# Expert row lists taken in two parts, the first two blocks started inside the routing, and the last two blocks added through a 0/1 product

## The chip, the cores and the metric

The kernel runs on one core of a Trainium2 chip. The metric is device time in microseconds (us) from launch to end; lower is better. Engines are named as in the profile: PE (TensorE matmuls) and PEld (its weight loads), DVE (VectorE), ACT (ScalarE), POOL (GpSimd), SP (SyncE, which issues most DMAs). Everything is float32 unless a tile says bf16.

## What is computed

One layer of a hybrid decoder on 512 prompt tokens and 8 decoding tokens: a mixer (attention and convolution), then a mixture of experts, then a last RMSNorm. The change touches only the part from the end of the mixer on:

```python
x = x + mods[2] * mix
h = rmsnorm(x, norm2_g) * (1.0 + mods[4]) + mods[3]
# hier_moe(h): softmax over 4 groups, top 1; top 2 of the 8 experts of that group
hid = silu(h @ w_gate[e]) * (h @ w_up[e])        # 1024 -> 256, each of 32 experts
y   = sum over the token's two experts of weight * (hid @ w_down[e])
x   = x + mods[5] * y
out = rmsnorm(x, final_g)
```

Each token has two (token, expert) pairs, 1040 in all. Every expert's weights are 3 MB (gate, up, down, 1 MB each), 32 experts, 96 MB.

## The kernel before, in words

**Mixer end.** Attention runs over four tiles of 128 tokens. Between its steps a written queue (`QUEUE`, `FILL`) slips in the output projection: `project(i, n)` (line 1250) makes half n of tile i's new x (`x1`), stores it to `xrow` in DRAM (line 1257), and adds up its squares; `rows(i)` (line 1272) then scales the tile by its 1/rms on ACT (line 1279), multiplies by `A2b` and adds `B2b` on POOL (lines 1280 and 1281), stores h to `hrow` in DRAM (line 1282), and calls `choose(i)` and `place(i)`.

**Routing.** `choose(i)` (line 1179) finds the two experts of each token of tile i on DVE as 0/1 rows `OH`, and has PE count how many earlier tokens chose each expert (`pps`, lines 1201 and 1202). `place(i)` (line 1204) turns that into a slot of a block of 64 rows: `Rs`, the 0/1 matrix of the slot within its block, and `kk`, `OH3`, for which block. After the last tile, lines 1437 to 1482 work out, from the counts of all experts, the table `T` of blocks: 52 blocks of 64 rows, of which the first 6 (`NF`) belong to fixed experts 26 to 31, the next eight to four experts with two blocks each (`HV`), 22 more to one expert each, and 16 spare ones are for what is left over, behind a branch. `px` (lines 1449 to 1454) is the PE product that sums the counts, copied at line 1464. Lines 1483 to 1499 make from this `gix`, the list of rows of `hrow` for each pair of blocks; `six` (line 1515) is where each row's result goes in `yrow`; `wtb` (line 1538) its weight; `exi` (line 1510) the number of the expert of each block, read by SP into a register (line 1570) to address the weight loads (line 1574).

**Blocks.** `run` (line 1646) goes through 36 blocks. For each pair of blocks `gather` (line 1584) fetches 128 rows from `hrow` by an indirect DMA from POOL, `turned` (line 1589) transposes them on PE in two halves, `up` (line 1601) multiplies by gate and up, `hidden` (line 1610) is Silu on ACT and a product on DVE, `flip` (line 1616) transposes, `down` (line 1625) multiplies by the down weights, scales by weight and mods[5] (line 1634, tile `ot`) and scatters the rows to `yrow` by an indirect DMA from POOL (line 1635). Block b's `down` comes after block b+1's `up`; a list `chain` fixes PE's order. Weights lie in a pool of 21 pages of 1 MB (`NPAGE`), which hold everything of that size: the six fixed experts are loaded ahead during attention (`fetch`, line 1061, 18 pages), the pages `mA`, `mB` hold h and its transposes, and `rt` the routing's tables. Each further expert takes three pages that have become free.

**End.** After the 36th block the 16 spare blocks stand behind a branch that is not taken with these inputs (`nxi`, lines 1688 and 1689). Then SP reads `yrow` back (line 1703: per tile of 128 tokens two halves of 0.5 MB, `yt`), DVE adds both to x (`xt`, lines 1712 and 1716), ACT sums the squares (line 1717), POOL takes the power -0.5 (line 1723), DVE scales (line 1735), and SP stores (line 1736). `sample` (line 1738) does the 8 decoding tokens on POOL.

The instructions of each engine stand in an order that the compiler's scheduler picks from the program's order and from its own estimate of when inputs are ready; each engine then works through its list strictly in order. `issue_after(x)` forces an instruction behind x on its engine.

Of the kernel before, what the change touches and what calls it, by code (L numbers as in the profile page):

```python
# [20 lines left out]
EPS = 1e-6  # L21
# [97 lines left out]
def layout(x):  # L119
# [57 lines left out]
    a["RC"] = _RC  # L177
    return a


def body(tc, I, O, dbg=lambda *a: None):
# [899 lines left out]
    yrow = dr.tile([4 * NT, 512], F32, name="yrow")  # L1081
    m5s = cp.tile([128, 256], F32, name="m5s")
# [77 lines left out]
    BO = box(3, 10, NBLK, half_=True)  # L1160
    OH3 = BO.rearrange("p f a b -> p (f a b)")[:, :960].rearrange("p (a b c) -> p a b c", a=10, b=3)
# [17 lines left out]
    def choose(i):  # L1179
# [17 lines left out]
        V.tensor_tensor(Cb[:, i], OH[:, i, 0], OH[:, i, 1], op=ALU.add)  # L1197
        pps[i] = tps("pps", (128, 32))
# [4 lines left out]

    def place(i):
        m = eb
        V.tensor_tensor(m, OH[:, i], pps[i].unsqueeze(1).to_broadcast([128, 2, 32]), op=ALU.mult)
        r, k, r_ = rk[:, 0, 2 * i:2 * i + 2], kk[:, 2 * i:2 * i + 2], rk[:, 1, 2 * i:2 * i + 2]
        V.tensor_reduce(r, m, axis=AX.X, op=ALU.add)
# [3 lines left out]
        for j in range(2):  # L1212
# [6 lines left out]
                        s3.unsqueeze(3).to_broadcast([128, 2, 3, 32]), op=ALU.mult)  # L1219
        V.scalar_tensor_tensor(k, k, -1.0, s3[:, :, 2], op0=ALU.mult, op1=ALU.mult)  # L1220
        if i == 4:
            V.tensor_scalar(k, k, K("inv"), None, op0=ALU.add)

# [26 lines left out]
    def project(i, n):  # L1250
# [5 lines left out]
        V.scalar_tensor_tensor(xh, pA, ra[:, 0, i:i + 1], xh, op0=ALU.mult, op1=ALU.add)  # L1256
        SP.dma_start(xrow[128 * i:128 * i + 128, 512 * n:512 * n + 512], xh)
# [14 lines left out]
    def rows(i):  # L1272
# [6 lines left out]
        hop = S.activation(h2, x1[i], AF.Copy, scale=rs2[:, i:i + 1])  # L1279
        G.tensor_tensor(h2, h2, A2b, op=ALU.mult)  # L1280
        G.tensor_tensor(h2, h2, B2b, op=ALU.add)
        SP.dma_start(hrow[128 * i:128 * i + 128, :], h2)
        choose(i)
        yield
        place(i)
# [38 lines left out]
    later = []  # L1324
    for i in range(4):
        if i < 3:
            split_q(i + 1)
        if i == WOC:
            load_wo(1, 3)
            w1_, w2_ = page("mA"), page("mB")  # L1330
            (m2b, A2b), (B2b, pqs) = [(half(t, 0), half(t, 1)) for t in (w1_, w2_)]
            h2b = [m2b, pqs]
# [104 lines left out]
    pct = tps("pct", (32, 1))  # L1437
# [16 lines left out]
    PE.matmul(px[:, 2, :], col(2), K("su")[:32, :33], start=True, stop=True)  # L1454
# [27 lines left out]
    V.scalar_tensor_tensor(T[:, 2], ov[:, :32], 1.0 - OV0, hB, op0=ALU.add, op1=ALU.add)  # L1482
# [294 lines left out]
```

## Time and profile before

| | us |
|---|---|
| median of three runs (804.25 to 809.23) | 806.44 |
| the profiled execution, own time | 798.72 |
| its span, first to last instruction | 796.9 |

Durations are from the profiled execution. PE is busy 88% of the span, DVE 56%, ACT and POOL 27% and 26%. The mean granted clock of TensorE is 0.938 of full speed. Times in rows are us from the span's start. The routing lies from about 497 to 525, the blocks from 524 to 760, the end from 760 to 797.

### The profile page before, as it was taken

To read this page: it belongs to the slowest core of one execution; us is meant where nothing else is said; L and a number is where in the kernel's file an instruction comes from. 1 tells how busy PE (TensorE), PEld (TensorE's weight loads), DVE (VectorE), ACT (ScalarE), POOL (GpSimd) and SP (SyncE) were. 2 spreads that over 40 slices of the span, in tenths; PEclk is the share of its full clock that TensorE was granted. 3 is DMA by queue.
4 is the path that set the end of the run, shared out by engine and by line. 5 is a ranking of instruction groups with operands and counts; after the bars stand their busy time and mean duration, and the time that the engine had idled before them with its cause. 6 is when DMAs were issued, how large, how long until landed. Compare 5 with 4: busy or idle time off the path is not lost. (4 is left out here: it accounts for less than half of the span.)

```text
span 796.9 us, 12648 instructions
## 1 busy us (share of the span) xinstructions
PE 698.6 (88%) x4888; PEld 419.3 (53%) x4888; DVE 443.9 (56%) x960; ACT 214.5 (27%) x491; POOL 210.8 (26%) x182
## 2 busy tenths in 40 slices
PE   4999898998969998999998998279999999999800
PEld 3555887876757446544443554255555555554400
DVE  3445629999973857553356757853333333333245
ACT  1254721211113447543435323110101101010011
POOL 5144205043202101014253034213222222321114
PEclk9999999999979998999997999579999999999965
DMA  9985325646867702520006575669999999999953
GB/s 344 419 332 201 135 80 214 240 159 238 271 238 303 278 2 76 229 106 1 0 2 239 199 276 206 243 204 410 419 416 351 402 419 418 417 420 419 368 196 152
DMA packets 42332, 200.02 MB, mean 251 GB/s; under 512 B 10733, under 2 KB 14205, under 8 KB 22677
## 3 DMA queue, kind: packets, MB, share of 16 engines
q1 hardware_dynamic: 29341, 156.27, 50.2%
q0 software_dynamic: 10336, 40.95, 13.2%
q10 hardware_dynamic: 2592, 1.95, 0.8%
q8 instruction: 40, 0.66, 0.3%
q14 instruction: 23, 0.19, 0.1%
HBM read 187.82 MB, written 22.15 MB: 263 GB/s over the span
## 5 line engine op out<-in xcount | busy, mean ns | idle before, releaser
L591 DVE SCALAR_TENSOR_TENSOR y<-u,c,y 128x511 f32<-128x511 f32 (+23 forms) x120 | 102.2, 884 | 2.1
L1613 ACT ACTIVATE hd<-pgu 64x256 f32<-64x256 f32 x36 | 13.6, 377 | 200.3 <-PE pgu L1608 200.3
L1635 POOL DMA_INDIRECT yrow<-ot,six x36 | 39.2, 1088 | 99.2 <-DVE ot L1634 87.6
L1608 PE MATMUL pgu<-eu,mB 128*64 128x256 f32 x256 | 61.8, 384 | 1.9 <-DMA eu<-in_WU 1.8
L1608 PE MATMUL pgu<-eg,mB 128*64 128x256 f32 x256 | 62.2, 384 | 0.0
L1630 PE MATMUL pd<-ed,hTe 128*64 128x512 f32 x240 | 57.3, 598 | 0.8 <-issue 0.8
L1608 PE MATMUL pgu<-eu,mA 128*64 128x256 f32 x224 | 54.0, 384 | 1.7 <-DMA eu<-in_WU 1.7
L1608 PE MATMUL pgu<-eg,mA 128*64 128x256 f32 x224 | 54.2, 384 | 0.0
L1634 DVE SCALAR_TENSOR_TENSOR ot<-pd,wtb,mt 128x512 f32<-128x512 f32 x36 | 27.0, 751 | 44.3 <-PE pd L1630 44.3
L1614 DVE TENSOR_TENSOR hd<-pgu,hd 64x256 f32<-64x256 f32 x36 | 15.4, 428 | 57.3 <-ACT hd L1613 57.3
L1608 PEld LDWEIGHTS pgu<-eg,mB 128*64 128x64 f32 x256 | 32.8, 136 | 19.8 <-issue 5.1
L225 DVE COPY hTe<-hTp 128x128 f32<-128x128 f32 x36 | 10.5, 292 | 50.1 <-PE hTp L1621 47.4
L1608 PEld LDWEIGHTS pgu<-eg,mA 128*64 128x64 f32 x224 | 28.9, 136 | 17.7 <-issue 5.2
L1367 DVE TENSOR_REDUCE ast<-pSp 128x1 f32<-128x384 f32 (+3 forms) x44 | 27.0, 633 | 20.1 <-PE pSp L1364 19.9
L1372 ACT ACTIVATE P<-pSp,ast 128x128 f32<-128x128 f32 (+3 forms) x64 | 33.1, 528 | 15.4 <-DVE ast L1367 13.7
L370 PE MATMUL pr<-cTs,wc 128*64 128x256 f32 x256 | 36.1, 390 | 0.0
L1608 PEld LDWEIGHTS pgu<-eu,mB 128*64 128x64 f32 x256 | 33.0, 137 | 3.9 <-DMA eu<-in_WU 2.8
L1253 PE MATMUL woA<-wo,qT 128*128 128x512 f32 x64 | 32.1, 606 | 0.0
L1391 PE MATMUL oT<-PTp,kv 128*64 128x512 f32 x80 | 31.9, 652 | 0.0
L1109 PE MATMUL woC<-wo,y 128*128 128x512 f32 x64 | 31.2, 605 | 0.0
L361 PE MATMUL cT<-CI,cR 128*128 128x128 f32 x128 | 21.1, 302 | 11.0 <-DVE cR L386 10.9
L1608 PEld LDWEIGHTS pgu<-eu,mA 128*64 128x64 f32 x224 | 28.9, 136 | 2.7 <-DMA eu<-in_WU 2.1
(572 smaller groups left out, 1680.2 us busy)
## 6 DMA issues: line engine op xcount, KB each, us to landing
eg<-in_WG SPq DMA_DIRECT2D x26, 1024.0 KB
eu<-in_WU SPq DMA_DIRECT2D x26, 1024.0 KB
ed<-in_WD SPq DMA_DIRECT2D x26, 1024.0 KB
wada<-in_WA SPq DMA_DIRECT2D x16, 1024.0 KB
wada<-in_WA POOLq DMA_DIRECT2D x8, 1024.0 KB
WG<-in_WG SPq DMA_DIRECT2D x6, 1024.0 KB
WU<-in_WU SPq DMA_DIRECT2D x6, 1024.0 KB
WD<-in_WD SPq DMA_DIRECT2D x6, 1024.0 KB
```

What stands on the lines that cost most here:

```text
L361: PE.transpose(p[:, j, :], R[b:b + n, c, k, 2 * s8:2 * s8 + 2, :], ident[b:b + n, b:b + n])
L370: mark["PE"] = PE.matmul(self.pr[r][64 * c:64 * c + 64], wc1[:, c, 8 * r + 4 * h + s, :], self.T[h][:, c, s], start=(h == 0 and s == 0), s ...
L591: V.scalar_tensor_tensor(yb[:, s_:CVS], ub[:, :CVS - s_], w(k), yb[:, s_:CVS], op0=ALU.mult, op1=ALU.add)
L1109: PE.matmul(p, zc[:, g, 128 * i:128 * i + 128], wo[2 * n + 1][:, g], start=(g == 0), stop=(g == 3))
L1253: PE.matmul(pA, oTp[:, g, 128 * i:128 * i + 128], wo[2 * n][:, g], start=(g == 0), stop=(g == 3))
L1367: V.tensor_reduce(st[k][:, 0, h0:h0 + nh], pS[k][:, :nh * L].rearrange("p (h l) -> p h l", h=nh), axis=AX.X, op=ALU.max, negate=True)
L1372: S.activation(P[k][:, g, :L], pS[k][:, o:o + L], AF.Exp, bias=st[k][:, 0, g:g + 1], accum_out=st[k][:, 1, g:g + 1])
L1391: PE.matmul(oT[64 * k:64 * k + 64, :], kv12[:, br - 1, kt, 128 + 64 * k:192 + 64 * k], PT[k], start=(br == 1 and kt == 0), stop=False)
L1608: chain[0] = PE.matmul(pgus[b][64 * h:64 * h + 64, :], xT[:, c, 64 * s_:64 * s_ + 64], w[:, c, :], start=(c == 0), stop=(c == 7))
L1630: chain[0] = PE.matmul(pd[64 * h:64 * h + 64, :], hT_[:, c, :], wd[:, c, 512 * h:512 * h + 512], start=(c == 0), stop=(c == 1))
L1634: V.scalar_tensor_tensor(ot, pd, wtb[:, b:b + 1], mt, op0=ALU.mult, op1=ALU.mult)
L1635: st = G.indirect_dma_start(out=yrow[:, :], out_offset=bass.IndirectOffsetOnAxis(ap=six[:, b:b + 1], axis=0), in_=ot, in_offset=None, boun ...
```

## The change

Six edits. (1) Only tiles 0 and 1 call `choose` and `place` as they go; `choose(2)` and `choose(3)` are called one after the other behind tile 3, and tile 3's h is made on PE: x times `A2b` beforehand (half on POOL, half on DVE), a diagonal matrix of the 1/rms, and `B2b` added by a one-row product. (2) The row lists of the six fixed experts (three pairs of blocks) are made by `static_part` and `static_rows` from tables `BS` of their own, straight after `choose(3)`, and the first gather is issued there. (3) PE transposes the first pair and runs `up(0)` between the parts of `px`, and `up(1)` behind the product for `exi`; `place(2)` and `place(3)` follow; `hidden(0)` stands behind `gix`, `hidden(1)` behind `wtb`. (4) `yrow` is filled with zeros early. (5) The branch stands behind `down` of block 33; `down` of blocks 34 and 35 keeps its rows in SBUF (`held`) instead of scattering them. (6) What the other blocks wrote is added to `xt` by eight DMAs from POOL with `accum_op=add`, issued behind the branch; the held rows are added by a PE product with a 0/1 matrix `oh` (token number against `tk`). Tile 3's 1/rms is made on ACT and DVE.

```diff
+            SP.dma_start(yrow.rearrange("(p a) (g f) -> p (a g) f", p=104, f=256), zr[:104].unsqueeze(1).to_broadcast([104, 40, 256]))
...
         V.scalar_tensor_tensor(xh, pA, ra[:, 0, i:i + 1], xh, op0=ALU.mult, op1=ALU.add)
+        if i == 3:
+            (V if n else G).tensor_tensor(h2b[1][:, 512 * n:512 * n + 512], xh, A2b[:, 512 * n:512 * n + 512], op=ALU.mult)
...
+            dg = small("dg", 128)
+            V.tensor_scalar(dg, ident, rs2[:, i:i + 1], None, op0=ALU.mult)
+            for n in range(2):
+                c, p = slice(512 * n, 512 * n + 512), lng("h2p")
+                PE.matmul(p, dg, h2[:, c], start=True, stop=False)
+                PE.matmul(p, one[0:1, 0:1].to_broadcast([1, 128]), B2b[0:1, c], start=False, stop=True)
+                evac(h2[:, c], p, eng="S")
+                SP.dma_start(hrow[128 * i:128 * i + 128, c], h2[:, c])
+        if i == 2:
+            return
+        if i == 3:
+            choose(2)
         choose(i)
...
+    def static_rows():
...
+        for i in (2, 3):
+            rank(i)
+            for j in range(2):
+                V.tensor_scalar(RsF[:, i - 2, j], K("slot"), r[:, i, j:j + 1], None, op0=ALU.is_equal)
+        pf = acc("pf", (128, NF))
+        for n, i in enumerate(order):
+            for j in range(2):
+                a = 2 * i + j
+                for f in range(2):
+                    chain[0] = PE.matmul(pf, RsF[:, i - 2, j] if i in (2, 3) else Rs[:, i, j], BS[:, f, a], start=(n + j + f == 0), stop=(n == 4 and j + f == 2))
+        gf = pf.rearrange("p (a s) -> p a s", s=2)
+        for s_ in range(2):
+            V.tensor_scalar(gix[64 * s_:64 * s_ + 64, 0:NF // 2], gf[64 * s_:64 * s_ + 64, :, s_], BIG, None, op0=ALU.add)
+        gather(0)
+    def static_part(i):
...
+        V.tensor_scalar(BS[:, 0, 2 * i:2 * i + 2], o, K("pio"), None, op0=ALU.mult)
+        V.tensor_scalar(BS[:, 1, 2 * i:2 * i + 2], o, 128.0 * i - BIG, None, op0=ALU.mult)
...
-    PE.matmul(px[:, 2, :], col(2), K("su")[:32, :33], start=True, stop=True)
+    turned(0, 0)
+    turned(0, 1)
+    with in_turn():
+        chain[0] = PE.matmul(px[:, 2, :], col(2), K("su")[:32, :33], start=True, stop=True)
+    up(0, at(ahead[0]), range(8))
+    first_up = chain[0]
...
+    with in_turn():
+        chain[0] = PE.matmul(pex, K("pio")[0:32], pe[:, :NE - NF], start=True, stop=True)
+    up(1, at(ahead[1]), range(8))
+    second_up = chain[0]
+    exi = cp.tile([1, NE - NF], I32, name="exi")
+    V.tensor_copy(exi, pex)
+    place(2)
+    place(3)
...
+    with tc.issue_after(gi.ins):
+        hop = hidden(0)
...
+    mark["V"] = V.tensor_copy(wtb, pb[:, 2])
+    rest.close()
+    with tc.issue_after(mark["V"].ins):
+        hop = hidden(1)
...
+        ot = held[:, b - OV0 + 2] if OV0 - 2 <= b < OV0 else mid("ot")
...
+        if OV0 - 2 <= b < OV0:
+            return
...
-    run(todo, asked)
+    before, W = run(todo[:-1], end=False), todo[-1][1]()
...
+    SP.dma_start(io, I["IO"].to_broadcast([128, 544]))
...
     with tc.If(nxv > 0):
...
+    for j in range(2):
+        for i in range(4):
+            G.dma_start(xt[i], ry[128 * i:128 * i + 128, 1024 * j:1024 * j + 1024], accum_op=ALU.add)
...
+    chain[0] = None
+    run([(OV0 - 1, lambda: W)], before)
+    with tc.issue_after(silu[1].ins):
+        for b in range(2):
+            V.tensor_scalar(oh[:, b], io, tk[:, b:b + 1], None, op0=ALU.is_equal)
...
     def total(i):
...
+        p = [acc("py") for _ in range(2)]
+        with in_turn():
+            for b, h in ((0, 0), (0, 1), (1, 0), (1, 1)):
+                chain[0] = PE.matmul(p[h], oh[parts[h], b, 128 * i:128 * i + 128], held[parts[h], b], start=(b == 0), stop=(b == 1))
+        for h in range(2):
+            xh = xt[i][:, 512 * h:512 * h + 512]
+            adds[0] = V.tensor_tensor(xh, p[h], xh, op=ALU.add)
+        r, s_ = rsf[:, i:i + 1], ssf[:, i:i + 1]
+        S.activation(jy, xt[i], AF.Square, scale=1.0 / 32, accum_out=s_)
...
+    total(0)
+    total(1)
+    final(0)
+    total(2)
+    final(1)
+    sample()
+    total(3)
+    final(2)
+    quarter_rstd(rsf[:, 4:5], fs, 1.0 / D, EPS)
+    final(3)
```

## Rows read from the trace of the kernel before

**Rows 1.** Busy time by stretch; last three columns: granted clock, DMA share, GB/s.
```profile
core 0: us, PE busy (x) PEld busy (x) DVE busy (x) ACT busy (x) POOL busy (x), PEclk, DMA share, GB/s
500.00:505.00 5.00, 2.10 (x16) 2.12 (x17) 3.53 (x8) 1.15 (x1) 3.66 (x3) 0.52 0.79 329
515.00:520.00 5.00, 1.64 (x27) 1.37 (x27) 3.64 (x18) 1.04 (x3) 1.12 (x1) 0.50 0.00 0
520.00:525.00 5.00, 2.35 (x34) 2.15 (x34) 4.75 (x18) 0.00 (x0) 1.01 (x1) 0.50 0.27 70
525.00:530.00 5.00, 5.00 (x36) 3.25 (x36) 1.66 (x5) 1.88 (x2) 0.99 (x1) 0.75 0.79 274
530.00:535.00 5.00, 5.00 (x46) 2.96 (x42) 0.92 (x3) 0.77 (x3) 0.00 (x0) 1.00 0.74 256
680.00:720.00 40.00, 40.00 (x292) 20.64 (x290) 14.05 (x28) 4.43 (x10) 9.87 (x9) 1.00 1.02 418
```

**Rows 2.** What PE waited for, 524 to 762 (in total, times, longest us).
```profile
PE pgu L1608 <- DMA eu<-in_WU: 3.5, 2, 1.8
```

**Rows 3.** Timeline of POOL and SP in the routing (start us, us, engine line op).
```profile
503.80 2.34 POOL L1281 TENSOR_TENSOR mB<-mB 128x1024 f32<-128x1024 f32 x1
518.74 1.12 POOL L1585 DMA_INDIRECT mA<-hrow,gix  x1 [12.60 <-DVE eb L1504]
...
524.55 0.35 SPq L1574 DMA_DIRECT2D eg<-in_WG  x1
...
530.47 0.34 SPq L1574 DMA_DIRECT2D eu<-in_WU  x1
```

**Rows 4.** Timeline of DVE in the routing.
```profile
502.10 1.67 DVE L1184 SCALAR_TENSOR_TENSOR rt<-rt,rs,bw 128x36 f32<-128x36 f32 x1
...
503.99 2.16 DVE L1174 SCALAR_TENSOR_TENSOR eq<-rt,RC 128x4 f32<-128x4 f32 x1
...
507.09 0.25 DVE L1174 SCALAR_TENSOR_TENSOR eq<-le,rt,RC 128x32 f32<-128x32 f32 x1
...
510.53 0.26 DVE L1464 COPY q<-px 128x99 f32<-128x99 f32 x1
...
519.61 0.17 DVE L1510 CAST exi<-pex 1x26 int32<-1x26 f32 x1
```

**Rows 5.** Timeline of the end: a scatter (block 33), last products and result, norm.
```profile
749.53 1.16 POOL L1635 DMA_INDIRECT yrow<-ot,six  x1 [6.04 <-DVE ot L1634]
...
757.67 1.94 PE L1630 MATMUL pd<-ed,hTe 128*64 128x512 f32 x8 [0.84 <-issue]
...
759.64 0.75 DVE L1634 SCALAR_TENSOR_TENSOR ot<-pd,wtb,mt 128x512 f32<-128x512 f32 x1 [1.62 <-PE pd L1630]
...
772.12 1.06 ACT L1717 ACTIVATE yt<-yt 128x1024 f32<-128x1024 f32 x1 [16.82 <-DMA yt<-yrow]
...
788.60 1.41 DVE L1735 SCALAR_TENSOR_TENSOR yt<-yt,rsf,gf 128x512 f32<-128x512 f32 x2
```

**Rows 6.** The chain that ended last (start us, us, what), its two longest pieces.
```profile
760.67 4.69 DMA yrow<-ot,six
...
766.75 6.96 DMA yt<-yrow
```

**Rows 7.** Timeline of PE: output projection, and transposes of the first pair.
```profile
494.52 1.96 PE L1253 MATMUL woA<-wo,qT 128*128 128x512 f32 x4
...
524.24 1.95 PE L1598 MATMUL xTp<-CI,mA 128*128 128x128 f32 x8
```

**Rows 8.** Busy time by stretch, during attention (columns as in rows 1).
```profile
330.00:340.00 10.00, 10.00 (x52) 5.58 (x53) 8.56 (x28) 7.44 (x26) 1.20 (x2) 1.00 0.02 8
```

**Rows 9.** Line 1689, the branch: PE's sequencer (ns min/median/max, start us).
```profile
L1689 PEldq COMPARE_BRANCH  x1: 4127/4127/4127, 758.3 to 758.3; - x1
```

**Rows 10.** Line 1773, the end of the program: POOL's drain (ns min/median/max, first and last start).
```profile
L1773 POOLq DRAIN  x3: 51/109/8257, 787.7 to 796.6; - x3
```

More of the change, by code (lines that the diff above doesn't have):

```diff
@@ new lines, in flip, with down @@
+    def flip(b):
+        hd = hds.pop(b)
+        pT = tps("hTp", (128, 2, 64))
+        with in_turn():
+            for c in range(2):
+                chain[0] = PE.transpose(pT[:, c, :], hd[64:128, 128 * c:128 * c + 128], ident[64:128, 64:128])
+        hTs_[b] = small("hTe", 128).rearrange("p (c t) -> p c t", c=2)
+        evac(hTs_[b], pT, eng="V")
+    def down(b, wd):
+        hT_ = hTs_.pop(b)
+        pd = acc("pd")
+        with in_turn():
+            for c, h in ((0, 0), (0, 1), (1, 0), (1, 1)):
+                chain[0] = PE.matmul(pd[64 * h:64 * h + 64, :], hT_[:, c, :], wd[:, c, 512 * h:512 * h + 512], start=(c == 0), stop=(c == 1))
+        ot = held[:, b - OV0 + 2] if OV0 - 2 <= b < OV0 else mid("ot")
+        V.tensor_scalar(mt, m5h, fl[:, 0, b:b + 1], fl[:, 1, b:b + 1], op0=ALU.mult, op1=ALU.add)
+        V.scalar_tensor_tensor(ot, pd, wtb[:, b:b + 1], mt, op0=ALU.mult, op1=ALU.mult)
+        if OV0 - 2 <= b < OV0:
+            return
+        st = G.indirect_dma_start(out=yrow[:, :], out_offset=bass.IndirectOffsetOnAxis(ap=six[:, b:b + 1], axis=0), in_=ot, in_offset=None,
+                                  bounds_check=4 * NT - 1, oob_is_err=False)
+        for o in scat:
+            tc.declare_no_dep(st.ins, o.ins, reason="rows of other slots")
+        scat.append(st)
@@ new lines, in in_turn, with run @@
+    def in_turn():
+        return tc.issue_after(chain[0].ins) if chain[0] is not None else ExitStack()
+    def run(blocks, before=None, end=True):
+        for n, (b, W) in enumerate(blocks):
+            W = W()
+            if n == 0 and b and b % 2 == 0:
+                turned(b // 2, 0)
+                turned(b // 2, 1)
+            if b > 1:
+                up(b, W, range(0, UP))
+            if before:
+                flip(before[0])
+            if b > 1:
+                up(b, W, range(UP, 8))
+            if b % 2 and n + 1 < len(blocks):
+                turned(b // 2 + 1, 0)
+            if b > 1:
+                hidden(b)
+            if before:
+                down(*before)
+            if b % 2 and n + 1 < len(blocks):
+                turned(b // 2 + 1, 1)
+            before = b, W[2]
+        if not end:
+            return before
+        flip(before[0])
+        down(*before)
@@ L1642, in in_turn @@
-    def in_turn():
-        return tc.issue_after(chain[0].ins) if chain[0] is not None else ExitStack()
-    def run(blocks, asks):
-        before = None
-        for n, (b, W) in enumerate(blocks):
-            W = W()
-            if n == 0:
-                turned(b // 2, 0)
-                turned(b // 2, 1)
-            up(b, W, range(0, UP))
-            if before:
-                flip(before[0])
-            up(b, W, range(UP, 8))
-            if b % 2 and n + 1 < len(blocks):
-                turned(b // 2 + 1, 0)
-            hidden(b)
-            if before:
-                down(*before)
-            if b % 2 and n + 1 < len(blocks):
-                turned(b // 2 + 1, 1)
-            before = b, W[2]
-        flip(before[0])
-        down(*before)
```

297 lines of the change are left out of this document (146 added, 151 removed).

## The prediction

> **What bounds the kernel now.** I read the busy time by stretch first, then the waits, then the timelines of the two places that the change touches, and last the chain that ended last. Over the blocks (680 to 720 stands for some 200 us) the DMA engines are full at 418 GB/s and PE is busy throughout [rows 1]. So the two are close; that DMA sets the pace at the end is shown by the only real wait of PE, 3.5 us for the last expert's weights [rows 2]. What starts this stream is the routing. From 515 to 520 nothing is transferred, from 520 to 525 a quarter of the engines work [rows 1]. The first weights of a chosen expert go out at 524.55 and the second at 530.47 [rows 3], although `exi` was there at 519.61 [rows 4]: pages were missing, not addresses. A page of 1 MB takes 2.5 us at 418 GB/s, so one early page and a gap amount to a stream that starts at 530.47 - 2.5 = 528.0. Behind the blocks comes an end of 796.9 - 760.4 = 36.5 us after the last `ot` (759.64 + 0.75 [rows 5]), which opens with two transfers in a row: the last scatter 4.69, the read back 6.96 [rows 6].
>
> **The change part by part: routing.** The row list for the first pair no longer waits for the block table. `choose(3)` held two instructions that stood beside POOL's products: line 1184 took 1.67 and line 1174 took 2.16, where a like one takes 0.25 [rows 4]; the last of these products ran to 506.14 [rows 3]. With tile 3's products off POOL that gives back up to 3.3 us. Against it stand a DVE product of some 0.75 (as line 1634 of the same size [rows 5]), up to 1.2 of stall beside the half product left on POOL (half of 2.34 [rows 3]) and four small `BS` instructions of 0.25 (rank and `RsF` are a part of what `place` did). `choose(2)` I cost at nothing: it hides in DVE's gaps while PE makes tile 3's projection; if the scheduler leaves it behind the 1/rms, it costs 3 to 4 us (a dozen instructions of 0.25 and up). So `choose(3)` ends about 507 instead of 509, and the list takes 2.3 more (rank, slots, 20 small products, `gix`): 509.5.
>
> The gather also needs tile 3's h in DRAM. On PE it costs four products of 512 columns; two such took 1.96 at full clock [rows 7], so four take 3.9 at full and 7.7 at the lower of the two clock levels, 1.2 GHz, which was granted from 500 on (0.52 [rows 1]). From about 502.7 that is 506.6 to 510.4, plus 0.6 for ACT's copy and 2 to land. I take 510.5 for the gather's issue, 8 us before 518.74 [rows 3]; bounds 509 and 513.
>
> Then the change gives part of it back. `px`'s last product, and with it line 1464, now stands behind the transposes of the first pair. The gather lands some 3.6 us after its issue (both gathers' bytes fall in 520 to 525 [rows 1, 3]), 514.1; the transposes take 1.95 [rows 7]; line 1464 runs at about 516.4 instead of 510.53. Everything that hangs on `T` is 6 us later. The product for `exi` moreover stands behind `up(0)`. Before, `up(0)` lay between 526.2, the end of the transposes, and 530.47, when its page came free [rows 3, 7], 4.3 us at a clock of 0.75 [rows 1]. I take 4.6, so `exi` at 521.6, 2 us later than before, and the first weights a us later, 522.6. But now two pages are free at once and two more after `up(1)`, about 525, then block 0's down page near 529: no gap. The stream starts at 522.6 against 528.0, **5.4 us earlier**. Bounds: 0 if `exi` comes at 527 (late `choose(2)`, or a gather held up by the prefetch that fills the engines to 515), 8 if h is written at full clock.
>
> PE must follow. Two `up`s are done ahead, but `hidden(0)` waits for the late `gix`, `hidden(1)` for `wtb`, and PE, in order, waits with them; by the same shifts block 2 starts near 531 rather than 537 and loses about a us to `flip(1)`. That is 4 to 6 us of gain on PE too, and PE had 3.5 us of waits to spare [rows 2], so DMA's 5.4 carries through. The zeros for `yrow` (4.26 MB, 10.2 us at 418 GB/s) go out during attention, where the engines are idle (0.02 from 330 to 340, and later stretches like it [rows 8]): nothing; uncovered they would cost the 10.2.
>
> The branch now lies between two blocks. DVE, ACT and POOL pass it in half a us, but PE's took 4.13 [rows 9]. It was hidden in the end; now `up(35)` stands behind it. PE's sequencer reaches it while `down(33)` still runs (it began at 758.3 beside products that ran from 757.67 to 759.61 [rows 5, 9]), and PE waited here for weights anyway. Bounds 0 and 4, I take 1. The last `ot` comes at 760.4 - 5.4 + 1 = **756.0**.
>
> **The change part by part: the end.** The last scatter and the read back leave the path; what is late next is the eight adding transfers. They start when the scatter of block 33 has landed: issue 749.53 [rows 5] less 5.4, plus 4.7 to 6 (4.69 for one alone [rows 6]), about 750. No row shows an adding transfer. Each moves 0.52 MB: 1.25 us at 418 GB/s if it runs like a plain one in a full stream [rows 1]; 4.69 to 6.96 from issue to landing [rows 6] if they run one at a time, which would be so if each waits for the one before. The second round waits tile by tile for the first, but four are always open, so I go from the plain row and double it, since the destination must be read as well as the source: 2.5 each, 20 us, the last landing at **772**.
>
> The Trainium skill (Collectives: The Full Stack, "The bandwidth ceiling: the fold count and why AG ≠ RS ≠ AR") says that a reducing transfer is slower not by the add but by its second source read, and gives half the rate of a copy; by it the eight would also take 20 us. No run here shows it yet.
>
> PE's 0/1 products (four of 512 columns per tile, as one `down`: 1.94 [rows 5], so 8 us and the sample's 16 short ones) run from 756 and are done by 767, before that landing. The last tile then needs two adds of 0.75 = 1.5, square and read 1.25 (1.06 and the read of the sum [rows 5]), 1/rms on ACT and DVE about 1.2 (six instructions of 0.15 to 0.25), two scalings 1.41 [rows 5]: 777.4. In the run before, 6.9 us lay between the last scaling, 790.0 [rows 5], and the end at 796.9; POOL's drain filled them (8.26 from 787.75 [rows 10]), and POOL's last work now comes earlier against the last scaling. I keep 5.6 of the 6.9: the span ends at **783.0**, 13.9 us sooner. The profiled execution's own 798.72 becomes 784.8; the median of the runs shown is 7.7 above that execution, so I put it at 806.44 - 13.9 = **792.5**.
>
> **Rivals.**
> A. *Adding transfers at the plain rate.* They land by 762, and the path is DVE's from 756.0: product 1.94, eight adds 6.0, four scalings 5.4, sample about 1.5, last square and 1/rms 2.5, less what overlaps, about 16.7. 772.7 + 5.6 = 778.3, gain 18.6: 787.8. For it: 4 KB rows like the plain read. Against it: twice the reads.
> B. *The routing gives nothing*: the new order on PE puts `px` and `exi` behind the gather, and what the list gains is eaten. Scatter, transfers and all that follows lie 5.4 later: gain 8.5, 797.9. For it: line 1464's 6 us. Against it: the page wait to 530.47.
> C. *Slower: the adding transfers run one at a time*, at the mean of the two pieces of the chain, 5.8 each: 46.4 us from 750, last landing 796.4, end 796.4 + 5.4 + 5.6 = 807.4, 10.5 later: 816.9. It decides from 4.5 us a transfer on (36 / 8). For it: POOL's queue and the waits of the second round; against it: POOL's scatters and gathers of different blocks ran beside a full weight stream all along.
> D. *The branch's 4.13 us show in full, and the clock falls behind them.* In the forecast this is hidden, since the transfers end last; with A it costs up to 5 us: 792.8.
>
> **How the numbers follow.** Forecast 0.43, A 0.22, D with A 0.05, B 0.18, C 0.08, other 0.04. A measurement of this kernel tells about 1%, 8 us, from no change. Faster by that: forecast, A and D nearly whole and half of B, 0.78; within: the rest of B, 0.13; slower: C and a part of the rest, 0.09. The range reaches from A with the routing's bound of 8 us (785) to B with transfers somewhat slower than half rate (803).
>
> **What would show it.** Right: first chosen weights issued near 522 with the next ones at once; line 1464 later than before, near 516; PE's branch of about 4 us before `up(35)`; the adding transfers landing over some 20 us after 750, the last tile's add waiting for them. Wrong: the first weights later than 527; adds waiting for PE and not for DMA (A); one landing every 4.5 us or more (C); a PE gap of over 3 us before `up(35)` with the clock at 0.5 behind it, and the last `ot` after 758 (D).

## The result, and the profile after

The changed kernel takes 826.76 us (median, 826.34 to 830.17) against 807.75 for the one before in the same comparison: ratio 1.025, 95% interval 1.020 to 1.030. That is slower by 19 us, where 13.9 less were forecast.

| | before | after |
|---|---|---|
| profiled execution, own time (span), us | 798.72 (796.9) | 826.52 (824.5) |
| mean granted clock | 0.938 | 0.929 |
| ACT's square of tile 2's second half (the sixth; "the mark"), us | 487.0 | 499.3 |
| mark to Silu of block 2, us | 54.4 | 62.6 |
| Silu of block 2 to the end, us | 255.4 | 262.6 |

The 27.6 us between the two profiled executions are thus 12.2 ahead of the mark, 8.2 from there to block 2, and 7.2 from block 2 to the end. The rows that these stretches are counted from, before and then after (ACT):

```profile
487.03 0.63 ACT L1258 ACTIVATE sqx<-x1b 128x512 f32<-128x512 f32 x1 [3.53 <-DVE x1b L1256]
...
541.45 0.38 ACT L1613 ACTIVATE hd<-pgu 64x256 f32<-64x256 f32 x1 [5.86 <-PE pgu L1608]
```

```profile
499.26 0.63 ACT L1301 ACTIVATE sqx<-x1b 128x512 f32<-128x512 f32 x1 [3.53 <-DVE x1b L1297]
...
561.89 0.38 ACT L1548 ACTIVATE hd<-pgu 64x256 f32<-64x256 f32 x1 [13.91 <-PE pgu L1543]
```

The first number needs care: over the profiled executions of this study whose queues begin as before, the mark lies anywhere between 483.9 and 501.6, and timed runs of the kernel before alone spread from 793.6 to 824.3. The other two repeat within about a microsecond where routing and end are the same, with one exception: the new routing brought block 2 to 62.6, 62.9 and 64.8 in three traces. So stretches are compared from the mark on, and what lies ahead of it is judged by timed runs alone. The stretches from the mark make 15.4 us, 1.9% of 807.75; the zeros, timed alone, 0.9% more (below). That is 2.8% for the 2.5% measured, inside its interval.

**Ahead of the mark.** SP's timeline of the changed kernel (start us, us, engine, line):

```profile
3.18 1.04 SPq L1389 DMA_DIRECT2D yrow<-zr  x1
```

The zeros for `yrow` stand in the program at the loads of `wo`, beside attention, where the engines are idle [rows 8]. They wait for nothing but a memset, and the scheduler put them at the head of SP's queue, at 3 us, among the first loads of the program.

**The routing.** First gather (POOL) and transposes (PE), then the first weights of a chosen expert (SP), then the table, block 0 and block 1 on DVE, and last the engines while PE waited and once the blocks run (timelines and windows of the changed kernel, the latter with the columns of [rows 1]; in a timeline the brackets hold the idle time ahead of an instruction and what ended it):

```profile
526.55 1.09 POOL L1262 DMA_INDIRECT mA<-hrow,gix  x1 [13.26 <-DVE gix L1251]
...
532.05 1.94 PE L1533 MATMUL xTp<-CI,mA 128*128 128x128 f32 x8 [6.64 <-DMA mA<-hrow,gix]
```

```profile
540.48 0.35 SPq L1513 DMA_DIRECT2D eg<-in_WG  x1
541.11 0.34 SPq L1513 DMA_DIRECT2D eu<-in_WU  x1
```

```profile
534.16 0.26 DVE L1649 COPY q<-px 128x99 f32<-128x99 f32 x1 [8.39 <-PE px L1637]
...
539.56 0.17 DVE L1679 CAST exi<-pex 1x26 int32<-1x26 f32 x1
543.73 0.37 DVE L1698 TENSOR_SCALAR gix<-ptb 64x23 int32<-64x23 f32 x2 [1.23 <-PE ptb L1693]
544.14 0.43 DVE L1549 TENSOR_TENSOR hd<-pgu,hd 64x256 f32<-64x256 f32 x1
550.23 0.21 DVE L1733 COPY wtb<-ptb 128x52 f32<-128x52 f32 x1 [0.68 <-PE ptb L1732]
...
552.62 0.29 DVE L224 COPY hTe<-hTp 128x128 f32<-128x128 f32 x1
...
556.73 0.75 DVE L1570 SCALAR_TENSOR_TENSOR ot<-pd,wtb,mt 128x512 f32<-128x512 f32 x1 [3.47 <-PE pd L1566]
```

```profile
545.00:550.00 5.00, 2.19 (x35) 1.82 (x34) 4.20 (x18) 2.56 (x5) 0.00 (x0) 0.76 1.01 426
550.00:555.00 5.00, 2.18 (x11) 0.89 (x10) 2.90 (x10) 0.00 (x0) 0.00 (x0) 0.50 0.93 360
...
650.00:655.00 5.00, 5.00 (x40) 2.61 (x38) 2.02 (x4) 0.38 (x1) 1.17 (x1) 1.00 1.01 413
```

These answer to [rows 3] and [rows 4]. Counted from the mark, the gather went out at 27.3 (before 31.7), but the copy of `px` came at 34.9 (before 23.5) and the rest of `gix` at 44.5 (before 31.0). `exi` came at 40.3 (before 32.6), and the first two weights of a chosen expert went out at 41.2 and 41.8 (before 37.5 and 43.4). From the rest of `gix` on DVE's queue holds everything: the weights, `wtb` 6.5 us behind `gix`, `hidden(1)`, the lists of what is left over, and only then `hTe`, for which PE, but for some transposes and the products of the weights, stood waiting since it had made `hTp` at 544.71. Between 545 and 555 PE worked 2.2 of 5 us and the clock fell to 0.50, so `down(0)` took 3.7 us instead of the 1.94 of a like one. From block 2 on PE is full, as it was before: Silu of block 2 to Silu of block 31 took 182.6 us before and after.

**The end.** The branch (duration in ns, start), the adding transfers and POOL's last work, the tiles on DVE, and the engines meanwhile (last columns of a window: clock, share of the DMA engines, GB/s):

```profile
L1779 PEldq COMPARE_BRANCH  x1: 6187/6187/6187, 767.9 to 767.9; - x1
...
L1779 POOLq INC_SWDGE_SEM  x1: 1956/1956/1956, 777.9 to 777.9; - x1
```

```profile
771.13 0.98 POOL L1573 DMA_INDIRECT yrow<-ot,six  x1 [6.08 <-DVE ot L1570]
780.64 2.97 POOL L1788 DMA_DIRECT2D xt<-yrow  x3 [8.53 <-DMA xt<-xrow]
...
795.26 0.87 POOL L1788 DMA_DIRECT2D xt<-yrow  x1 [1.48 <-DMA xt<-yrow]
...
815.16 0.55 POOL L335 TENSOR_TENSOR rsf<-rsqt,mh 128x1 f32<-128x1 f32 x1 [5.49 <-DVE rsf L1829]
```

```profile
797.58 1.29 DVE L1816 TENSOR_TENSOR xt<-py,xt 128x512 f32<-128x512 f32 x2 [10.84 <-DMA xt<-yrow]
...
800.98 1.28 DVE L1835 SCALAR_TENSOR_TENSOR xt<-xt,rsf,gf 128x1024 f32<-128x1024 f32 x1 [0.69 <-POOL rsf L1821]
802.18 1.28 DVE L1816 TENSOR_TENSOR xt<-py,xt 128x512 f32<-128x512 f32 x2
...
809.71 1.28 DVE L1835 SCALAR_TENSOR_TENSOR xt<-xt,rsf,gf 128x1024 f32<-128x1024 f32 x1 [0.44 <-POOL rsf L1821]
810.91 1.28 DVE L1816 TENSOR_TENSOR xt<-py,xt 128x512 f32<-128x512 f32 x2
...
815.18 1.42 DVE L1835 SCALAR_TENSOR_TENSOR xt<-xt,rsf,gf 128x512 f32<-128x512 f32 x2
```

```profile
790.00:795.00 5.00, 0.00 (x0) 0.00 (x0) 0.00 (x0) 0.00 (x0) 1.73 (x2) 0.84 1.10 212
795.00:800.00 5.00, 1.67 (x4) 1.31 (x6) 1.29 (x2) 1.05 (x2) 0.87 (x1) 0.50 1.08 212
...
805.00:810.00 5.00, 0.67 (x4) 0.00 (x0) 4.38 (x10) 1.15 (x2) 1.23 (x2) 1.00 0.31 123
```

```profile
L1888 POOLq DRAIN  x3: 51/109/8518, 815.1 to 824.2; - x3
```

These answer to [rows 5, 6, 9, 10]. The first adding transfer goes out 9.5 us behind the last scatter. The eight fill the engines at 187 to 212 GB/s, half of the weights' rate, until about 805, when the last one lands (the traffic falls between 800:805, 243 GB/s with the first output in it, and 805:810). Tile 3's adds, however, start only at 810.91: DVE scales tile 0 ahead of tile 1's adds and tile 2 ahead of tile 3's, and in both places it first waits for a 1/rms. POOL's last instruction is the 1/rms of the 8 decoding tokens at 815.16, and POOL's drain, 8.5 us from 815.1 on, ends the program.

### The profile page after: what moved, and what is told of

It reads as the page before. It is cut to its first block, busy times and chain, and to the rows that moved or that the text cites. A ratio compares the mean times of both kernels' runs of the same rounds, so it can differ in the third digit from the quotient of the medians.

```text
span 824.5 us, 12868 instructions
## 1 busy us (share of the span) xinstructions
PE 733.5 (89%) x4980; PEld 436.9 (53%) x4980; DVE 440.8 (53%) x988; ACT 219.1 (27%) x496; POOL 205.1 (25%) x184
## 5 line engine op out<-in xcount | busy, mean ns | idle before, releaser
L1543 PE MATMUL pgu<-eg,mB 128*64 128x256 f32 x256 | 64.2, 394 | 4.5 <-PEq L1779 4.5
L1543 PE MATMUL pgu<-eu,mB 128*64 128x256 f32 x256 | 64.0, 394 | 0.1
L1573 POOL DMA_INDIRECT yrow<-ot,six x34 | 36.7, 1079 | 91.6 <-DVE ot L1570 87.1
L369 PE MATMUL pr<-cTs,wc 128*64 128x256 f32 x256 | 37.9, 406 | 0.0
L224 DVE COPY hTe<-hTp 128x128 f32<-128x128 f32 x36 | 10.4, 290 | 46.3 <-PE hTp L1557 43.5
L1110 PE MATMUL woC<-wo,y 128*128 128x512 f32 x64 | 31.2, 605 | 0.0
```

The lines of the kernel that those rows point to most:

```text
L369: mark["PE"] = PE.matmul(self.pr[r][64 * c:64 * c + 64], wc1[:, c, 8 * r + 4 * h + s, :], self.T[h][:, c, s], start=(h == 0 and s == 0), s ...
L1110: PE.matmul(p, zc[:, g, 128 * i:128 * i + 128], wo[2 * n + 1][:, g], start=(g == 0), stop=(g == 3))
L1543: chain[0] = PE.matmul(pgus[b][64 * h:64 * h + 64, :], xT[:, c, 64 * s_:64 * s_ + 64], w[:, c, :], start=(c == 0), stop=(c == 7))
L1573: st = G.indirect_dma_start(out=yrow[:, :], out_offset=bass.IndirectOffsetOnAxis(ap=six[:, b:b + 1], axis=0), in_=ot, in_offset=None, boun ...
```

## The experiments

All stretches are read from one profiled execution each; times are counted from the mark. "New routing" is edits 1 to 3 of the change, "new end" edits 4 to 6. "gix rest" is the start of the second of the two instructions that write the rest of `gix`, 0.2 behind the start that a row of the timeline gives for the pair. Ratios are to the kernel before on the same chip, with their 95% interval, where a run was timed in rounds.

| run | gix rest | Silu of block 2 | from there to the end | mark to end | ratio |
|---|---|---|---|---|---|
| before | 31.2 | 54.4 | 255.4 | 309.9 | |
| after | 44.7 | 62.6 | 262.6 | 325.2 | 1.025 (1.020 to 1.030) |
| e1_fill_late | 44.8 | 62.9 | 263.0 | 325.9 | 1.015 (1.004 to 1.025) |
| e2_fill_alone | | | | | 1.009 (1.003 to 1.016) |
| e14_fill_late_alone | 31.2 | 54.7 | 255.7 | 310.3 | 0.997 (0.993 to 1.001) |
| e3_old_tail | 46.6 | 64.8 | 254.5 | 319.2 | 1.020 (1.009 to 1.031) |
| e4_new_tail | 31.2 | 54.9 | 262.6 | 317.5 | 1.010 (1.001 to 1.020) |
| e5_table_first | 44.5 | 62.5 | 255.7 | 318.2 | |
| e6_h_on_pool | 41.2 | 59.2 | 254.6 | 313.8 | |
| e13_flip_first | 41.4 | 53.8 | 256.1 | 309.9 | 0.993 (0.989 to 0.996) |
| e9_list_alone | 31.7 | 52.1 | 257.0 | 309.1 | 0.999 (0.992 to 1.005) |
| e7_no_branch | 31.2 | 54.4 | 257.5 | 311.9 | |
| e8_tail_order | 31.2 | 54.4 | 257.4 | 311.8 | |
| e10_plain_write | 31.2 | 55.0 | 252.4 | 307.3 | |
| e11_list_and_end | 31.7 | 52.1 | 254.9 | 307.1 | 0.991 (0.986 to 0.996) |
| e12_repaired | 43.4 | 61.7 | 257.1 | 318.8 | 1.018 (1.008 to 1.028) |
| e15_both | 41.3 | 53.6 | 255.6 | 309.2 | 0.993 (0.985 to 1.001) |

**The three parts by themselves.** e1 holds the zeros back until the loads before them are out; e2 is the kernel before with the zeros alone; e3 has the new routing alone, e4 the new end alone. The edit of e1 (in the quoted diffs the operands of a call are cut to their names):

```diff
-            SP.dma_start(yrow, zr)
+            with tc.issue_after(last.ins):
+                SP.dma_start(yrow, zr)
```

> The changed kernel with one edit: the DMA of zeros to yrow is held on SP behind the load of mB, so that it goes out during attention. Theory F: in the changed kernel the scheduler put this DMA, which waits for nothing, at the start of SP's queue (3.18 us); it shares the engines with the first loads, the first pieces come 5.7 us later, and the two stretches of lower clock that follow (230 to 253 and 325 to 338) are longer because everything stands 6 us later; 13 us in all by 343 us. It expects 826.8 - 13 = 814, first ACT work at 24 us as in the kernel before. If the lower clock has nothing to do with the fill, 5.7 come back: 821. Rival H, that the zeros are hidden as predicted and the late start has another cause: 827, with everything still 13 us late at 343.

> The kernel before with the zero tile and the DMA of zeros to yrow alone added, where the change has it (the scheduler puts it at the start of SP's queue). Theory F: 807.8 + 5.7 = 813.5 at least and 821 if the longer stretches of lower clock come with it. Rival H, that the zeros are hidden: 808.

> The changed kernel with the end of the kernel before: no zeros, no held blocks, all 36 blocks scattered, the branch behind block 35, plain reads. What is left of the change is the early row lists, tile 3's h on PE, and the first two blocks inside the routing. Theory R: PE paces blocks 2 to 33 (12.65 us a pair in both traces), so what counts is when block 2 starts, and that is 7 to 8 us later by the routing alone (its Silu 541.4 before, 561.9 after, 13 of these 20.5 from ahead of it): 807.8 + 8 = 816. Rival P, the prediction's own routing term: 5.4 us earlier, 802. Rival N, the routing neither gains nor loses: 808.

> The kernel before with the new end alone: zeros held back to attention, blocks 34 and 35 kept in SBUF, the branch between blocks 33 and 34, adding transfers, 0/1 products; routing as before. Theory T: from the product of block 33 to the end the changed kernel took 824.5 - 770.9 = 53.6 us, the one before 796.9 - 749.3 = 47.6; the new end costs 6: 814. Rival Q, the prediction's own term for the end: 8 to 9 us gained, 799.

The zeros alone at the head of the queue cost 0.9% (2 to 13 us). In e1 the time fell to the side that was expected (1.015), but the interval overlaps that of the change, and its four executions spread from 813.7 to 829.4. The second half of theory F, that the longer stretches of low clock ahead of the mark are due to the zeros, is not borne out: the profiled execution of e4, without zeros at the start, has longer ones than before too (last section). The new routing alone brings block 2 to 64.8, 10.4 us later than before, where theory R gives 7 to 8, and not 5.4 early. The new end alone takes 262.6 from block 2, as in the change, 7 to 8 more than the old one, and theory T's 814 is met (813.5).

**What makes the routing late.** All three on e3_old_tail (old end). e5 makes the table first, and the transposes and `up` of the first pair behind `exi`:

```diff
-    turned(0, 0); turned(0, 1); up(0)
...
-    up(1)
...
     V.tensor_copy(exi, pex)
+    turned(0, 0); turned(0, 1); up(0); up(1)
...
```

> The run e3_old_tail (new routing, old end) with the products for the block table first: px's last product and the one for exi stand ahead of the transposes and of up(0), not behind them, and the later routing products are no longer forced behind up(0) and up(1). Times from the square of tile 2's second half (the sixth). Before: table copy 23.5, exi 32.6, first chosen weights 33.4 and 37.5 to 38, gix's rest 31.2, Silu of block 2 at 54.4. With the new routing (three traces): table copy 34.6 to 36.4, exi 40.3 to 42.2, Silu of block 2 62.6 to 64.8. Theory R1: it is the table's wait for the first pair's gather that costs, on both sides; table copy 23 to 24, exi 27 to 29, weights at once behind it, 12 us earlier than with the new routing; the gix rest still stands behind up(1) on PE (about 42), so block 2 gains only what PE gains, 3 to 4 us: Silu of block 2 at 59 to 61, total 4 less than e3_old_tail. Rival R2, that the weight stream sets the pace from block 2 on: its 12 us carry through, Silu of block 2 at 52.

In e5 the copy of `px` came at 25.4 and `exi` at 28.3, where e3 had it at 42.2. The first weights of a chosen expert nevertheless went out at 40.3 (e3: 43.1), in the moment in which block 0's Silu began and a page came free; SP's timeline, and ACT's at block 2:

```profile
527.18 0.35 SPq L1512 DMA_DIRECT2D eg<-in_WG  x1
```

```profile
549.44 0.38 ACT L1547 ACTIVATE hd<-pgu 64x256 f32<-64x256 f32 x1 [13.93 <-PE pgu L1542]
```

So the addresses were there 14 us earlier, but R2's condition, weights right behind `exi`, never came about: pages were missing. Block 2 stood 18.0 behind the rest of `gix`, as in e3 (18.2), and both came 2.1 to 2.3 earlier. That is no more than traces of the same routing differ by (62.6 in the change). So the addresses of the weights don't set the pace; block 2 follows the row lists. What an earlier stream itself would do, no run shows; from block 2 to block 31 PE had no wait for it to shorten.

e6 takes h of tile 3 off PE, as the other tiles have it:

```diff
...
+        S.activation(h2, x1[i], AF.Copy, scale=rs2[:, i:i + 1])
+        G.tensor_tensor(h2, h2, A2b, op=ALU.mult)
+        G.tensor_tensor(h2, h2, B2b, op=ALU.add)
...
```

> The run e3_old_tail with tile 3's h made as before (ACT's scaling, POOL's product and sum, one store), all else of the new routing kept. With the new routing the four products of h took 7.7 us of PE at the lower clock, the rank's counts stood behind them, and the first gather went out 26.9 to 27.6 after the sixth square. Theory R1: the h products on PE cost nothing net against POOL's two passes of 2.1 to 2.3 us and ACT's 1.1, of which choose's stalls come back: gather 26 to 29, Silu of block 2 within 1.5 us of 62.6 to 64.8. Rival R3, that PE's products of h are what makes the new routing late: gather at 23 to 24 and Silu of block 2 at 59 or earlier.

Rival R3 was nearer: gather at 24.7, block 2 at 59.2, 5.6 less than e3 and 3.4 less than the change. The rest stayed: 18.0 from `gix` to block 2. e13 goes on from e6 and turns the hidden part of block 0 ahead of the weight lists:

```diff
-            if before:
+            if before and before[0]:
                 flip(before[0])
...
         hop = hidden(0)
+    with tc.issue_after(hop.ins):
+        flip(0)
```

> The run e6_h_on_pool with one edit: the transposes of block 0's hidden rows and their copy (hTe) stand straight behind hidden(0), ahead of the weight lists, not behind hidden(1) and the lists of what is left over. With the new routing Silu of block 2 came 17.9 to 18.3 us after the gix rest in every trace (6.3 of them to wtb, then hidden(1), 2 us of lists, the copy hTe, down(0) at the lower clock, up(2)); before it was 23.2 after it, but the gix rest came 10 to 15 us earlier. Theory C: DVE's queue holds PE there: hTe needs only hidden(0) and up(1) and can be 4 us behind the gix rest instead of 8.7; Silu of block 2 12 to 14 us behind it, at 53.5 to 55.5, 4 to 5 earlier than in e6_h_on_pool. Rival: PE itself fills that stretch with up(1) and down(0) at the lower clock: 17 to 18 behind the gix rest again.

DVE and then ACT, e6_h_on_pool:

```profile
533.30 0.37 DVE L1682 TENSOR_SCALAR gix<-ptb 64x23 int32<-64x23 f32 x2 [1.28 <-PE ptb L1677]
...
542.20 0.29 DVE L226 COPY hTe<-hTp 128x128 f32<-128x128 f32 x1
...
551.50 0.38 ACT L1534 ACTIVATE hd<-pgu 64x256 f32<-64x256 f32 x1 [13.95 <-PE pgu L1529]
```

and e13_flip_first:

```profile
536.06 0.37 DVE L1682 TENSOR_SCALAR gix<-ptb 64x23 int32<-64x23 f32 x2 [1.32 <-PE ptb L1677]
...
537.38 0.29 DVE L226 COPY hTe<-hTp 128x128 f32<-128x128 f32 x1 [0.20 <-PE hTp L1543]
...
548.67 0.38 ACT L1534 ACTIVATE hd<-pgu 64x256 f32<-64x256 f32 x1 [8.37 <-PE pgu L1529]
```

One copy of 0.29 us, moved from 8.9 to 1.3 behind `gix`, brings block 2 from 18.0 to 12.4 behind it: theory C. With h off PE and this order the new routing is level with the old one (53.8 against 54.4).

**What is early worth by itself.** The old routing with the early list alone:

> The kernel before with one part of the change, the early list of rows: the tables of the six fixed experts are filled behind each tile's slots, their list (20 small products) is made straight after the last tile's slots, and the first gather goes out there. All else stays as before: each tile chooses as it goes, h of tile 3 on ACT and POOL, the block table's products, gix and exi ahead of the first pair on PE, one change only: up(0) stands ahead of the weight products. Times from the sixth square; before: gather 31.7, gix rest 31.2, first chosen weights 33.4, Silu of blocks 0, 1, 2 at 43.5, 47.4, 54.4 (four traces within 0.6). Theory R1, that PE paces the blocks and that the new routing lost by putting the table behind the gather: here the gather goes out at 27 to 28, the gix rest at 32, Silu of block 0 at 38 to 40 and of block 2 at 50 to 52, 3 to 4 us earlier than before; the total gains 2 to 4 us at most, since the weights at the end come only as early as pages come free. Rival R4, that a gather issued early is held up by the weights loaded ahead and lands no earlier: Silu of block 2 at 54 to 55, total as before.

The first gather went out at 26.1 and block 2 came at 52.1, 2.3 earlier, but from there to the end it took 1.6 more than before: the last weights went out 1.3 us earlier, block 33 came 1.3 earlier, and the end behind it was 0.5 longer. Timed, no difference. Here the table and `gix` stand ahead of the first pair on PE, and the rest of `gix` came at 31.7, as before, against 41.2 in e6, which has h off PE too. So the early list does not put `gix` back; the order around it does.

**What makes the end late.** All on e4_new_tail; e7 leaves out the branch and the spare blocks behind it, e8 holds DVE's scalings behind the next tile's adds (below), e10 (on e8) leaves out the sums of the eight transfers.

```diff
-    total(0); total(1); final(0); total(2); final(1)
-    sample(); total(3); final(2); quarter_rstd(...); final(3)
+    total(0); total(1)
+    for i in range(3):
+        with tc.issue_after(adds[0].ins):
+            final(i)
+            if i == 1: sample(); quarter_rstd(...)
+        if i < 2: total(i + 2)
+    final(3)
```

> The run e4_new_tail without the branch and the 16 spare blocks behind it (they do nothing with these inputs). From Silu of block 33 to the end the new end takes 63.2 to 64.9 in three traces, the old one 55.0 to 58.1. Theory T1: the branch joins the engines: POOL waits there for all scatters and then takes 2.0 us to reset its queues, PE stands 4.5 us before up(35), and the first adding transfer goes out 9.5 us after the last scatter. Without it: first adding transfer 5 to 6 us after the last scatter's issue, no gap of PE beyond DVE's, 55 to 58 us to the end if the transfers start the earlier by that, 7 less. Rival T2, that the half rate of the adding transfers and DVE's chain behind them set the end wherever they start and the branch is hidden: 63 to 65 still.

> The run e4_new_tail with the order at the end forced: on DVE the adds of the next tile ahead of the scaling of the one before, and the 8 decoding tokens' 1/rms ahead of tile 3's. In the changed kernel the last adding transfer ends by 804, yet tile 3's adds start at 810.9, since DVE does three scalings and the sample in between, and POOL's drain of 8.5 us begins only behind the sample's 1/rms at 815.1. Theory T3: DVE's order and that drain cost the end about 4: last scaling 4 to 5 earlier, Silu of block 33 to the end 59 to 61 instead of 63.2 to 64.9. Rival T2', that the transfers alone set it: adds of tile 3 wait for DMA and the end stays at 63 to 65.

> The run e8_tail_order with the eight transfers from yrow to xt writing instead of adding (the sum over yrow and the x rows is left out; the work and the waits behind them stay). Theory T5: an adding transfer takes twice the time of a plain one, 2.4 us against 1.25 each when the engines are full; the eight then take 10 to 12 us instead of the 20 to 22 that the changed kernel shows (780.6 to about 804, at 187 to 212 GB/s with the engines full), and from Silu of block 33 to the end it takes 51 to 54 instead of 58.7. Rival T6, that the rate comes from the issue by POOL or from the 4 KB rows of yrow: 187 to 212 GB/s again, and no change.

e8 gave 5 us back (257.4 against 262.6), a little more than T3 said; DVE now has tile 3's adds ahead of tile 2's scaling:

```profile
783.99 1.28 DVE L1743 TENSOR_TENSOR xt<-py,xt 128x512 f32<-128x512 f32 x2
785.25 1.28 DVE L1762 SCALAR_TENSOR_TENSOR xt<-xt,rsf,gf 128x1024 f32<-128x1024 f32 x1
```

e7 gave as much, and by the number T1 would stand. The rows say otherwise:

```profile
759.05 1.40 POOL L1645 DMA_INDIRECT yrow<-ot,six  x1 [6.04 <-DVE ot L1642]
767.34 2.06 POOL L1710 DMA_DIRECT2D xt<-yrow  x2 [6.89 <-DMA xt<-xrow]
```

```profile
787.86 1.29 DVE L1738 TENSOR_TENSOR xt<-py,xt 128x512 f32<-128x512 f32 x2 [2.35 <-DMA xt<-yrow]
789.07 1.27 DVE L1757 SCALAR_TENSOR_TENSOR xt<-xt,rsf,gf 128x1024 f32<-128x1024 f32 x1
```

The first adding transfer still waited 8.3 us behind the last scatter (9.1 in e4), because it needs the scatter landed and the x rows read. What changed is DVE's list: without the branch the scheduler itself put tile 1's adds ahead of tile 0's scaling. The last adding transfer landed 44.2 us behind Silu of block 33 in e7 and 45.3 in e4; from that landing to the end it took 15.0 and 19.5 (14.0 in e8). So the branch is worth about 1 us here, and the rest of e7's gain lies where e8's does.

Windows of e10 (sums left out) and of e8:

```profile
771.00:774.00 3.00, 3.00 (x16) 1.02 (x14) 0.75 (x1) 0.00 (x0) 1.02 (x2) 1.00 1.02 345
...
777.00:780.00 3.00, 0.79 (x3) 0.48 (x5) 1.29 (x2) 0.16 (x1) 0.53 (x1) 0.93 0.99 388
```

```profile
767.00:770.00 3.00, 0.00 (x0) 0.00 (x0) 0.00 (x0) 0.00 (x0) 1.04 (x2) 1.00 1.10 214
...
773.00:776.00 3.00, 0.78 (x2) 0.68 (x4) 1.29 (x2) 0.15 (x1) 0.00 (x0) 0.50 1.09 214
```

While the engines were full, the same eight transfers ran at 308 to 388 GB/s when they write (774:777 has the 308) and at 180 to 214 when they add (180 and 186 from 761 to 767); from the first landing to the last it took 11.2 and 18.7 us, and the end is 5 us shorter. T5 holds and T6 falls, but the price of the sum is 1.7 times here, not twice.

**Together.** e12 joins e1, e5, e6 and e8; e14 is the zeros held back alone; e11 is e9 with POOL off the old end's last step (Sqrt on ACT and four small instructions on DVE in place of POOL's power, and the 1/rms of the decoding tokens ahead of tile 3); e15 is e13 with that end. The edit of e11 and e15:

```diff
-ORD, ISS = "t0 t1 f0 t2 f1 s t3 q f2 f3", "fsq"
+ORD, ISS = "t0 t1 f0 t2 f1 s q t3 f2 f3", "fsq"
...
-        G.tensor_tensor(r, r, mh[:, 0:1], op=ALU.pow)
```

> The changed kernel with four edits of the runs before together: the zeros held back (e1), tile 3's h on ACT and POOL (e6), the table's products ahead of the first pair (e5), the order at the end forced (e8). The theory that these four carry the loss adds up what each run gave: the zeros 0.9% of 806, 7 us (e2), h 3.4 (Silu of block 2 at 59.2 against 62.6 in the changed kernel), the table 2.3 (e5 against e3_old_tail), the order 6.2 (e8 against e4): 19 of the 19 us between the medians. It expects 808, a ratio to the kernel before of 0.995 to 1.01, Silu of block 2 at 56 to 58 and 58 to 59.5 from Silu of block 33 to the end. Rival: the parts share one cause, so that together they give no more than the largest two: 813 to 816, a ratio of 1.01 or more.

> The kernel before with the zeros for yrow alone, held on SP behind the load of mB so that they go out during attention. Theory F: held back they are hidden: a ratio to the kernel before of 0.995 to 1.004, where the start of the queue gave 1.009. Rival: they cost wherever they go out (4.26 MB beside the loads of wo and x): 1.006 to 1.013.

> The run e9_list_alone with the end of the kernel before kept (plain reads, branch behind block 35), except that POOL leaves the last step: the 8 tokens' 1/rms stands ahead of tile 3's, and tile 3's is made on ACT and DVE. In the kernel before POOL's drain of 8.26 us begins with its last instruction (787.75) and ends at 796.05, 2.4 us after the last wait of SP for an output (793.5). Theory T3: the end follows POOL's last instruction by 8.3 to 8.5; with it 2 to 4 us earlier the end comes 1 to 2.4 us earlier than in e9_list_alone, from Silu of block 33 to the end 54 to 56.5 against 55 to 58. Rival T4, that the output's transfers set it: no gain, or 1 us slower by the five small instructions.

> The run e13_flip_first with the end of e11_list_and_end (old end, the 8 tokens' 1/rms ahead of tile 3's, tile 3's on ACT and DVE). Theory: the two gains lie in different stretches and add: Silu of block 2 at 53.5 to 54.5 after the sixth square as in e13_flip_first, from Silu of block 33 to the end 2 to 3 us less than the 55.2 there, POOL's drain no longer last; a ratio to the kernel before of 0.985 to 0.992. Rival: the weights, which come last in e13_flip_first too (PE waits for them behind block 33), take back what the order gives, and only the end's 3 us show: 0.993 to 0.998.

e12 fell short: the end is mended (257.1), but block 2 came at 61.7. The gains of e5 and e6 don't add, since with the table first the rest of `gix` stands behind `up(1)` (43.4) and the 18 us behind it stay; that is what led to e13. e14 shows the zeros free where the program has them. e11 is the fastest here: 307.1 from the mark, 2.8 us or 0.35% less than before, and 0.9% by timing (0.4 to 1.4%), which is more than its stretches explain; its end ran 2.1 us shorter than e9's. e15 is not told apart from the kernel before. e13 is level with it by the stretches though timed at 0.993; e14, which only adds work, was timed at 0.997, so I take neither as faster. No run joins e13's routing with e8's end; by their stretches that would be 53.8 + 257.4 = 311.2 from the mark, 1.3 more than before.

## Why the prediction was wrong, step by step

- **"DMA sets the pace at the end ... the stream starts 5.4 us earlier."** This is the step that failed first. The 3.5 us in [rows 2] belong to the last blocks alone. From block 2 to block 31 PE is full before and after, and e5 put the addresses 14 us earlier for at most 2.3 us of block 2. The term should have been the start of PE's block 2, and I gave it one sentence. Nor did the stream start earlier: `exi` came 7.7 us later against the mark, not 2, as the gather gained 3.8 less than forecast and took 1.9 more to land, and the first two weights went out at 41.2 and 41.8, where my count for the kernel before (528.0) is 41.0.
- **"PE must follow ... 4 to 6 us of gain on PE too."** It lost 8.2. I named the order (`hidden(0)` behind `gix`, `hidden(1)` behind `wtb`) and priced it by the shift of `px`, not by what is queued behind it on DVE: `hTe` behind the weights cost 5.4 to 5.6 us (e13), h on PE 3.4 to 5.6 (e6).
- **The list itself.** `choose(3)` was right: it ended 2.7 us earlier against the mark (518.85 against 509.29), without the stalls of [rows 4]. The gather was forecast 8.2 us earlier and came 4.4 earlier. h on PE took 8.1 us (514.55 to the second copy at 522.65), as [rows 7] gives at the low clock (7.7); and rank, which I had beside it, stood behind those products on PE (`pps` at 522.54), so that the list came 2.9 behind them. The landing took 5.5, not 3.6. The late copy of `px` I had seen, at 6 us; it was 11.4.
- **"The zeros ... nothing."** Wrong by the place: they don't go out where the program has them. At the head of the queue they cost 0.9% (e2), within the 10.2 us that I gave for uncovered ones; held back they are free, as forecast (e14).
- **The adding transfers** were right in size: 2.5 each forecast; the eight landed between 786.5 and 805.0, 2.6 apart, and e10 shows that it is the sum that costs the rate, 1.7 times. The Trainium skill (Collectives: The Full Stack, "The bandwidth ceiling: the fold count and why AG ≠ RS ≠ AR") says that ReduceScatter runs at half of AllGather's rate because its add needs two source reads. It says so of collectives over several ranks, not of a transfer on one core; the rates here, 180 to 214 against 308 to 388 GB/s, are of that size, and whether the read or the add costs it no run here shows.
- **"Start about 750, 6 behind the scatter"** was 9.5 behind it: POOL waited 6.7 for the scatter's landing and then 1.96 for the reset of its queues at the branch. The x rows, which I left out, were as late: read beside the last weights, they landed from 779.6 on, so that without the branch it was still 8.3 (e7).
- **"After that 5.4 + 5.6"** failed, and it is the larger miss at the end: 19.6 us lie between the last landing and the end. The 5.4 held for one tile alone; DVE, in order, did four tiles (e8: 5 of it). And the end is not 5.6 behind the last scaling but follows POOL's drain, 8.5 from POOL's last instruction on, which the change made late, not early. From the scatter of block 33 to the end I had forecast 38.9, where the kernel before took 47.3; it took 53.4: 3.6 more at the start of the transfers, 2.3 in them, 8.6 behind them.
- **The branch:** 6.19 us on PE, 4.5 of them idle, clock at about 0.5 behind it, as rival D said, and hidden, as the forecast said.
- **Rivals.** B was right about the mechanism of the routing and stopped at "nothing". C alone had the sign, with 10.5 of the 19 us, for a mechanism that isn't there: the transfers ran side by side at a lower rate.

## What to carry to other kernels

Before costing an earlier start, ask which engine is full in the stretch that follows, and count to its first instruction there, through everything that stands ahead of it in each engine's list. An instruction that waits for nothing can go to the head of its queue, as the zeros did, and not where the program has it, and a chain at the end is the sum over all tiles on the engine that works in order, not one tile's chain.

## What the hardware showed that I had not expected

- POOL's drain at the end of the program began with its last instruction in every trace and took 8.26 us with the old end and 8.52 with the new one, 8.96 in e11 and 9.49 in e10, whose ends have POOL's last instruction earlier. In every trace but e11's and e15's the end came 0.9 us behind the drain's; so there POOL's last instruction, of 0.55 us before and after, set the end.
- Two executions, like work on PE, and a low clock of different length behind an idle stretch: before, PE idled for 7.4 us until 231.87 and was at full clock again in 240:245; after, it idled for 7.3 until 238.10 and was still at 0.50 in 245:250, with PE full since 240. First before, then after:

```profile
235.00:240.00 5.00, 5.00 (x36) 3.77 (x34) 2.28 (x3) 2.33 (x6) 0.00 (x0) 0.77 0.00 0
240.00:245.00 5.00, 5.00 (x43) 4.82 (x44) 1.13 (x2) 1.05 (x5) 2.39 (x3) 1.00 0.24 56
```

```profile
240.00:245.00 5.00, 5.00 (x20) 3.76 (x18) 2.74 (x4) 1.62 (x3) 0.00 (x0) 0.50 0.02 3
245.00:250.00 5.00, 5.00 (x29) 4.31 (x28) 1.28 (x3) 2.06 (x5) 0.00 (x0) 0.50 0.00 0
```

These are windows as in [rows 1]. That alone is 4 us between two profiles, with no part of the change in it: e4, whose queue begins as before, lost the same 4 us there. What decides the length stays open.
